# One PSUM pool of eight banks, half-size weight tiles and an earlier fourth weight sum in a transformer encoder block

## The chip, the cores and the metric

The kernel runs on one core of a Trainium2 chip. The metric is the device time of one execution in microseconds (us). Every number ahead of the prediction comes from the kernel before the change: from its three timed runs or from one execution taken by the hardware profiler. In the profile, PE is TensorE (matmuls), PEld its weight loads, DVE is VectorE, ACT is ScalarE, POOL is GpSimd and SP is the engine whose queue issues most DMAs. In the timeline each engine's instructions stand in the order of its program, so an instruction that waits holds up all that stand behind it on that engine.

## What is computed

One encoder block on 256 tokens of width 2048, in float32. What matters here is the tail of it and the matmul work:

```python
h = rms_norm(x, g_mix);  proj = h @ w_in            # q, k, v of three mixers, and three gates
...                                                 # three attentions; memory tokens: rms_norm(mem) @ w_mem_kv
merged = gates[0] * (oa @ w_br_a) + gates[1] * (ob @ w_br_b) + gates[2] * (oc @ w_br_c)
x = x + merged @ w_o
hf = rms_norm(x, g_ffn) @ w_ffn_in                  # 2048 x (2 * 5632)
x = x + (silu(hf[..., :D_FF]) * hf[..., D_FF:]) @ w_ffn_out
```

## The kernel before

Weights stream from HBM once, in tiles of up to 128 x 4 x 512 (`raw`, 1 MB, three slots). A float32 product is made from three matmuls on rounded halves: `split` lets ACT write the high part `whi` (line 86) and DVE the rest `wlo` (line 87) of a 128 x 2 x 512 half, and PE then adds high x high, high x low and low x high for each 128-row tile. `whi` and `wlo` have four slots each, so ACT runs at most four halves ahead of PE.

The stages follow each other on PE: two `w_mem` column blocks, eight `w_qkv` blocks with the attention heads worked in beside them (`tick` advances side jobs between matmuls), twelve pairs of gate and branch products with the merge, four `w_o` blocks, and the FFN. `product` (lines 161 to 188) makes one 512-wide column block into two PSUM banks, one per 128 tokens (`ps[0]`, `ps[1]`). `transposed` (lines 223 to 237) turns a finished block with eight PE transposes into two banks `tp` and splits the result for the next product.

The FFN's input product runs in eleven blocks through `in_seven` (lines 525 to 615). A block makes the two factors of 512 hidden columns for both token halves. For three pairs of k tiles (steps `s0` to `s2`) it uses seven products in place of eight, from sums of the weights (`t2`, `t3`, `t4`, made by DVE) and of the activations (`fh`, `fl`). The other five pairs (`d3` to `d7`) are done plainly. `ORDER` lists the steps of a block: `6`, `7` and `4` are the products with `t2`, `t3` and `t4`, over all three pairs at once. The partial sums are in banks X, Y, Z, W, V and Q. Y, V, Z and Q take the plain steps; X serves three sums one after the other, which ACT copies out. At a block's end DVE combines banks and copies into SA and SB (lines 609 to 614), ACT applies Silu (line 623), DVE multiplies (line 624), and `transposed` turns the product for `w_ffn_out`. A group of blocks (4, 4 and 3) is followed by four `w_ffn_out` products over that group, added to `x` (line 637).

PSUM has eight banks. Up to `w_o`, pool `mm` holds four (products) and pool `at` four (attention, transposes). For the FFN both are closed and opened anew as seven and one (lines 503 to 505).

The order of instructions on each engine is made by the framework's scheduler from program order and data dependencies. A tile gets one of its pool's slots as the scheduler places its first writer.

Of the kernel before, what the change touches and what calls it, by code (L numbers as in the profile page):

```python
# [11 lines left out]
F32 = mybir.dt.float32  # L12
# [15 lines left out]
PK, LOAD = 2, 4  # L28
# [24 lines left out]
ORDER = "s0 d3 s1 d4 s2 d5 6 d6 7 d7 4".split()  # L53
ORDER0 = "d3 d4 d5 s0 s1 d6 s2 6 d7 7 4".split()
# [3 lines left out]
def encoder_block(ctx: ExitStack, tc: tile.TileContext, a: dict, out: bass.AP):  # L58
# [7 lines left out]
    banks = ExitStack()  # L66
    pools = {"mm": banks.enter_context(tc.tile_pool(name="pmm", bufs=4, space=bass.MemoryType.PSUM)),
             "at": banks.enter_context(tc.tile_pool(name="pat", bufs=4, space=bass.MemoryType.PSUM))}
# [7 lines left out]
    def at_bank(name):  # L76
        return pools["at"].tile([P, NC], F32, name=name, tag="at")

    def mm_bank(name="mm"):
        return pools["mm"].tile([P, NC], F32, name=name, tag="mm")  # L80
# [69 lines left out]
    def load(src, k0, nk):  # L150

        raw = wp.tile([P, LOAD, NC], F32, name="raw")
        if nk % PK:
            c = k0 % PK * NC
            nc.sync.dma_start(out=raw[:, 0], in_=src[k0 // PK][:, c:c + NC])
        else:
            nc.sync.dma_start(out=raw[:, :nk].rearrange("p (u k) n -> p u (k n)", k=PK),
                              in_=src[k0 // PK:(k0 + nk) // PK].rearrange("u p n -> p u n"))
        return raw

    def product(src, lhs, nk, head=(), beside={}):


        ps = [mm_bank() for _ in range(T)]
        k0 = 0
        while k0 < nk:
            n = head[0] if head else min(LOAD, nk - k0)
# [5 lines left out]
            for b in range(0, n, PK):  # L173
                m = min(PK, n - b)
                hi = wp.tile([P, PK, NC], F32R, name="whi", bufs=4)
                lo = wp.tile([P, PK, NC], F32R, name="wlo", bufs=4)
                split(hi[:, :m], lo[:, :m], raw[:, b:b + m])
                for i in range(m):
                    k = k0 + b + i
                    xh, xl = lhs(k)  # L180
                    for t in range(T):
                        c = slice(t * P, (t + 1) * P)
                        nc.tensor.matmul(ps[t], lhsT=xh[:, c], rhs=hi[:, i], start=(k == 0), stop=False)  # L183
                        nc.tensor.matmul(ps[t], lhsT=xh[:, c], rhs=lo[:, i], start=False, stop=False)  # L184
                        nc.tensor.matmul(ps[t], lhsT=xl[:, c], rhs=hi[:, i], start=False, stop=(k == nk - 1))  # L185
                    tick()
            k0 += n
        return ps
# [34 lines left out]
    def transposed(src, dst, g=None):  # L223

        for h in range(2):
            tp = at_bank("tp")
# [40 lines left out]
    def biases():  # L267
# [7 lines left out]
        for g in range(3):  # L275
# [4 lines left out]
            ps = at_bank("bias_ps")  # L280
# [19 lines left out]
    def take_slots(ps, slots, r, name="x", eng=nc.gpsimd):  # L300
# [38 lines left out]
        if n:  # L339
# [14 lines left out]
            for j in range(n):  # L354
                tp = at_bank("hT")
# [10 lines left out]
    def attend(qs, ks, vs, bias, kt):  # L366
# [5 lines left out]
        for i in range(g):  # L372
            sc = at_bank("sc")
# [29 lines left out]
        def turn(i):  # L403
            tp = at_bank("pT")
# [9 lines left out]
        ops = at_bank("o")  # L414
# [27 lines left out]
    first = product(a["w_mem"][0], memT, KT, (1, 1) + (2,) * 7, {6: row_sums(a["mem"], r_m, 3, "mem")})  # L442
# [3 lines left out]
    start(take_slots(product(a["w_mem"][1], memT, KT, (2,) * 8), MEM_SLOTS[4:], r_m, "mem"))  # L446
# [78 lines left out]
    def in_seven(src, lhs, forms, order):  # L525
# [5 lines left out]
        dest = {"s": "XYZW", "6": "X", "7": "X", "4": "V"}  # L531
        left = {}
        for o in order:
            for b in ([dest["s"][0], "Y", "Z", "W"] if o[0] == "s" else ["Y", "V", "Z", "Q"] * 2 if o[0] == "d"
                      else [dest[o]] * SEVEN):
                left[b] = left.get(b, 0) + 1
# [4 lines left out]
        def mul(b, st, hi, lo):  # L541
            first = b not in ps
            if first:
                ps[b] = mm_bank("mm" + b)
# [7 lines left out]
        def halves():  # L552
            hi = wp.tile([P, PK, NC], F32R, name="whi", bufs=4)
            lo = wp.tile([P, PK, NC], F32R, name="wlo", bufs=4)
            return hi, lo
# [7 lines left out]
        t4 = s8([P, SEVEN, NC], "t4", F32)  # L563
        for o in order:
            if o[0] in "sd":
                u = int(o[1])
                raw = wp.tile([P, LOAD, NC], F32, name="raw")
                nc.sync.dma_start(out=raw.rearrange("p k n -> p (k n)"), in_=src[u])
            if o[0] == "d":
                for c in range(2):  # L570
                    hi, lo = halves()
                    split(hi, lo, raw[:, 2 * c:2 * c + 2])
# [4 lines left out]
            elif o[0] == "s":  # L577
                hi, lo = halves()
                split(hi, lo, raw[:, :2])
                mul("X", at(2 * u, 0), hi[:, 0], lo[:, 0])  # L580
                mul("Y", at(2 * u + 1, 0), hi[:, 1], lo[:, 1])
                hi, lo = halves()
                nc.vector.tensor_add(t3[:, u], raw[:, 2], raw[:, 3])
                nc.vector.tensor_add(raw[:, 2], raw[:, 2], raw[:, 0])
                split(hi, lo, raw[:, 2:])
                mul("W", forms(u, 0), hi[:, 0], lo[:, 0])
                mul("Z", forms(u, 2), hi[:, 1], lo[:, 1])
                nc.vector.tensor_add(t2[:, u], raw[:, 2], raw[:, 3])
                nc.vector.tensor_add(t4[:, u], t2[:, u], raw[:, 1])
                tick()  # L590
                if left["X"] == 2 * SEVEN:
                    nc.scalar.activation(SA[:, 0], ps["X"], AF.Copy)
                if left["W"] == 0:
                    nc.scalar.activation(SA[:, 1], ps["W"], AF.Copy)
            else:
                tt, f = {"6": (t2, 1), "7": (t3, 3), "4": (t4, None)}[o]
                for v in range(0, SEVEN, 2):
                    n = min(2, SEVEN - v)
                    hi, lo = halves()
                    split(hi[:, :n], lo[:, :n], tt[:, v:v + n])  # L600
                    for i in range(n):
                        u = v + i
                        mul(dest[o], at(2 * u + 1, 1) if f is None else forms(u, f), hi[:, i], lo[:, i])
                tick()
                if o == "6":
                    nc.scalar.activation(SB[:, 0], ps["X"], AF.Copy)
                elif o == "7":
                    nc.scalar.activation(SB[:, 1], ps["X"], AF.Copy)
        nc.vector.tensor_sub(SB[:, 0], SB[:, 0], SA[:, 1])
        nc.vector.tensor_sub(SA[:, 1], SA[:, 1], SB[:, 1])  # L610
        nc.vector.tensor_add(SA[:, 0], ps["Y"], SA[:, 0])
        nc.vector.tensor_add(SB[:, 1], ps["V"], SB[:, 1])
        nc.vector.tensor_sub(SB[:, 0], ps["Z"], SB[:, 0])
        nc.vector.tensor_add(SA[:, 1], ps["Q"], SA[:, 1])
        return (SA[:, 0], SB[:, 1]), (SB[:, 0], SA[:, 1])

    forms = stationary_forms()
    for c0, c1 in ((0, 4), (4, 8), (8, KF // 4)):
        hT = []
        for n in range(c0, c1):  # L620
            av, bv = in_seven(a["w_ffn"][n], x1l, forms, ORDER0 if n == 0 else ORDER)
            for t in range(T):
                nc.scalar.activation(av[t], av[t], AF.Silu, scale=r_f[:, 0, t:t + 1])
                nc.vector.scalar_tensor_tensor(av[t], bv[t], r_f[:, 0, t:t + 1], av[t],
                                               op0=ALU.mult, op1=ALU.mult)
            tl = s8([P, 2, 4, S], "hT", pool=tail)
            hT.append(tl)
            transposed(av, lambda k, m: (tl[:, 0, k:k + m], tl[:, 1, k:k + m]))
# [51 lines left out]

def _layout(i):
# [37 lines left out]
```

## Time and profile before

| | us |
|---|---|
| three timed runs, median (lowest to highest) | 1429.48 (1427.87 to 1429.51) |
| the profiled execution, its own time | 1432.02 |
| its span, first to last instruction | 1430.2 |
| PE busy in the span | 1400.4 |
| PE idle in the span | 29.8 |
| DVE, ACT busy | 963.3, 741.0 |

A group's row in the views gives the line, the engine, the operation, what is written from what, its shapes and its count; then busy time and mean duration in ns, and behind the bar the idle time of that engine just ahead of such instructions with what ended it. Matmuls overlap in the pipe: a 128x512 one is recorded with 389 ns while the next starts after some 228 ns, so spacing is read from starts. PEclk, or the granted clock, is the share of full speed that TensorE was given.

### The profile page before, as it was taken

What the parts mean: (1) busy time and instruction counts of PE and PEld (TensorE: products, weight loads), DVE (VectorE), ACT (ScalarE), POOL (GpSimd) and SP (SyncE); (2) the same over time, 40 slices, a digit from 0 to 9 for tenths busy, and PEclk for the clock granted to TensorE, in tenths of its full rate; (3) what the DMA queues carried; (4) which work ended last, traced back from release to release, by engine and by line L of the source; (5) the groups of instructions that cost most, each with busy time, mean ns of one, the idle gap of its engine ahead of it and who ended that gap; (6) DMA issues with size and microseconds to landing.
All of it is one profiled execution on the core that took longest, in us unless ns stands there. A gap on an engine that the chain in (4) does not pass through costs nothing.

```text
span 1430.2 us, 16503 instructions
## 1 busy us (share of the span) xinstructions
PE 1400.4 (98%) x6323; PEld 1151.6 (81%) x6323; DVE 963.3 (67%) x1191; ACT 741.0 (52%) x971; POOL 78.8 (6%) x146
## 2 busy tenths in 40 slices
PE   6999999999999999999899999999999999999998
PEld 4778788888888888888687788888888888888887
DVE  5666776754455555555688987557988855788763
ACT  5576556544444444444456555435655643456542
POOL 0012642200000000000000000000000000000000
PEclk8999999999999999999999999999999999999999
DMA  8876445456555555655455554555554555655562
GB/s 293 272 255 187 147 175 176 135 218 217 195 180 202 191 169 188 213 181 179 174 177 180 211 186 188 187 195 206 201 186 176 203 206 190 222 176 178 206 223 101
DMA packets 64510, 276.99 MB, mean 194 GB/s; under 512 B 5232, under 2 KB 7792, under 8 KB 52912
## 3 DMA queue, kind: packets, MB, share of 16 engines
q1 hardware_dynamic: 61984, 271.73, 54.8%
q10 hardware_dynamic: 2448, 4.22, 0.9%
q8 instruction: 49, 0.80, 0.2%
q14 instruction: 29, 0.24, 0.0%
HBM read 273.05 MB, written 2.88 MB: 193 GB/s over the span
## 4 chain that ended last, share of the span: by engine, by line
PE 89%; DMA 4%; POOL 2%; DVE 2%; ACT 2%; issue 1%; SPq 0%; ACTq 0%; DVEq 0%; POOLq 0%
PE mm L184 18%; PE mm L183 18%; PE mm L185 18%; PE mmY L549 2%; PE mmY L550 2%; PE mmY L548 2%; PE mmZ L549 2%; PE mmZ L550 2%; PE mmZ L548 2%; PE mmV L549 2%; PE mmV L550 2%; PE mmV L548 2%; PE mmQ L550 2%; PE mmQ L549 2%; PE mmQ L548 2%; PE mmX L549 1%
## 5 line engine op out<-in xcount | busy, mean ns | idle before, releaser
L87 DVE TENSOR_TENSOR wlo<-raw,whi 128x1024 fp32r<-128x1024 f32 (+1 forms) x497 | 612.6, 1238 | 393.4 <-ACT whi L86 392.1
L86 ACT ACTIVATE whi<-raw 128x1024 fp32r<-128x1024 f32 (+1 forms) x497 | 524.0, 1061 | 573.5 <-PE mm L185 367.1
L183 PE MATMUL mm<-whi,xT 128*128 128x512 f32 x640 | 250.6, 393 | 1.4 <-ACT whi L86 1.1
L184 PE MATMUL mm<-wlo,xT 128*128 128x512 f32 x640 | 250.2, 391 | 1.1 <-DVE wlo L87 1.1
L185 PE MATMUL mm<-whi,xT 128*128 128x512 f32 x640 | 249.5, 391 | 0.0
L183 PEld LDWEIGHTS mm<-whi,xT 128*128 128x128 f32 x640 | 120.1, 188 | 26.7 <-ACT whi L86 1.6
L184 PEld LDWEIGHTS mm<-wlo,xT 128*128 128x128 f32 x640 | 120.2, 188 | 26.3 <-DVE wlo L87 1.5
L185 PEld LDWEIGHTS mm<-whi,xT 128*128 128x128 f32 x640 | 120.2, 188 | 24.6
L184 PE MATMUL mm<-wlo,hT 128*128 128x512 f32 x352 | 138.0, 393 | 0.0
L185 PE MATMUL mm<-whi,hT 128*128 128x512 f32 x352 | 137.6, 393 | 0.0
L183 PE MATMUL mm<-whi,hT 128*128 128x512 f32 x352 | 134.9, 391 | 0.0
L184 PEld LDWEIGHTS mm<-wlo,hT 128*128 128x128 f32 x352 | 66.1, 188 | 14.8
L183 PEld LDWEIGHTS mm<-whi,hT 128*128 128x128 f32 x352 | 66.1, 188 | 14.6
L185 PEld LDWEIGHTS mm<-whi,hT 128*128 128x128 f32 x352 | 66.1, 188 | 13.6
L87 DVE TENSOR_TENSOR wlo<-t,whi 128x1024 fp32r<-128x1024 f32 x66 | 62.9, 955 | 6.3 <-ACT whi L86 3.6
L548 PE MATMUL mmY<-whi,x1T 128*128 128x512 f32 x143 | 57.7, 403 | 5.6 <-DVE rs_h L96 5.6
L86 ACT ACTIVATE whi<-t 128x1024 fp32r<-128x1024 f32 x66 | 55.6, 843 | 10.9 <-PE mmX L550 5.7
L549 PE MATMUL mmY<-wlo,x1T 128*128 128x512 f32 x143 | 56.7, 397 | 0.1
L550 PE MATMUL mmY<-whi,x1T 128*128 128x512 f32 x143 | 56.3, 393 | 0.0
L548 PE MATMUL mmV<-whi,x1T 128*128 128x512 f32 x143 | 56.2, 393 | 0.0
L549 PE MATMUL mmV<-wlo,x1T 128*128 128x512 f32 x143 | 55.9, 391 | 0.0
L550 PE MATMUL mmV<-whi,x1T 128*128 128x512 f32 x143 | 55.9, 391 | 0.0
(192 smaller groups left out, 2117.5 us busy)
## 6 DMA issues: line engine op xcount, KB each, us to landing
raw<-in_w_ffn SPq DMA_DIRECT2D x88, 1024.0 KB, 4.9
raw<-in_w_gate SPq DMA_DIRECT2D x48, 1024.0 KB, 5.0
raw<-in_w_ffn_out SPq DMA_DIRECT2D x44, 1024.0 KB, 5.0
raw<-in_w_qkv SPq DMA_DIRECT2D x32, 1024.0 KB, 5.0
raw<-in_w_o SPq DMA_DIRECT2D x16, 1024.0 KB, 4.9
raw<-in_w_br SPq DMA_DIRECT2D x8, 1024.0 KB, 5.0
raw<-in_w_mem SPq DMA_DIRECT2D x15, 512.0 KB, 4.7
raw<-in_w_br SPq DMA_DIRECT2D x8, 512.0 KB, 3.5
```

The costliest lines, as they stand in the source:

```text
L86: nc.scalar.activation(hi, src, AF.Copy)
L87: nc.vector.tensor_sub(lo, src, hi.bitcast(F32))
L183: nc.tensor.matmul(ps[t], lhsT=xh[:, c], rhs=hi[:, i], start=(k == 0), stop=False)
L184: nc.tensor.matmul(ps[t], lhsT=xh[:, c], rhs=lo[:, i], start=False, stop=False)
L185: nc.tensor.matmul(ps[t], lhsT=xl[:, c], rhs=hi[:, i], start=False, stop=(k == nk - 1))
L548: nc.tensor.matmul(ps[b], lhsT=st[0], rhs=hi, start=first, stop=False, skip_group_check=chain)
L549: nc.tensor.matmul(ps[b], lhsT=st[0], rhs=lo, start=False, stop=False, skip_group_check=chain)
L550: nc.tensor.matmul(ps[b], lhsT=st[1], rhs=hi, start=False, stop=stop, skip_group_check=chain)
```

## The change

* All stages draw from one PSUM pool of eight banks under one tag (`bank`). Closing and reopening pools ahead of the FFN goes.
* `raw` becomes a half tile (128 x 2 x 512, 0.5 MB) with six slots in place of three full ones; each load is a DMA of its own. The FFN weights are laid out so that both factors' halves alternate (`_pairs`).
* The product with the fourth weight sum (`t4` before, step `4` at a block's end) is made for each pair at once, in its `s` step, from a sum written over the raw weights. It goes into bank V. `t4` and step `4` go.
* W is copied to SB, the second X sum to SB, the third to SA; the six combinations change accordingly.
* The FFN's row scale `r_f` stays in Silu but leaves the product: `av * bv` is one 128 x 1024 multiplication over both token halves, and `r_f` is applied where the output products are added to `x`.

The core of the diff:

```diff
-ORDER = "s0 d3 s1 d4 s2 d5 6 d6 7 d7 4".split()
-ORDER0 = "d3 d4 d5 s0 s1 d6 s2 6 d7 7 4".split()
+ORDER = "s0 d3 s1 d4 s2 d5 6 d6 7 d7".split()
+ORDER0 = "d3 d4 d5 s0 s1 d6 s2 6 d7 7".split()
...
-    pools = {"mm": banks.enter_context(tc.tile_pool(name="pmm", bufs=4, space=bass.MemoryType.PSUM)),
-             "at": banks.enter_context(tc.tile_pool(name="pat", bufs=4, space=bass.MemoryType.PSUM))}
+    psum = ctx.enter_context(tc.tile_pool(name="psum", bufs=8, space=bass.MemoryType.PSUM))
...
+    def bank(name):
+        return psum.tile([P, NC], F32, name=name, tag="bank")
...
     def load(src, k0, nk):
-        raw = wp.tile([P, LOAD, NC], F32, name="raw")
...
+        raw = wp.tile([P, PK, NC], F32, name="raw", bufs=6)
+        c = k0 % PK * NC
+        nc.sync.dma_start(out=raw[:, :nk].rearrange("p k n -> p (k n)"), in_=src[k0 // PK][:, c:c + nk * NC])
...
-    banks.close()
-    pools["mm"] = ctx.enter_context(tc.tile_pool(name="pm2", bufs=7, space=bass.MemoryType.PSUM))
-    pools["at"] = ctx.enter_context(tc.tile_pool(name="pa2", bufs=1, space=bass.MemoryType.PSUM))
...
             elif o[0] == "s":
...
+                b1, b2 = raws
+                hi, lo = halves(b1)
                 mul("X", at(2 * u, 0), hi[:, 0], lo[:, 0])
                 mul("Y", at(2 * u + 1, 0), hi[:, 1], lo[:, 1])
...
-                nc.vector.tensor_add(t2[:, u], raw[:, 2], raw[:, 3])
-                nc.vector.tensor_add(t4[:, u], t2[:, u], raw[:, 1])
                 tick()
+                nc.vector.tensor_add(b1[:, 1], t2[:, u], b1[:, 1])
+                hi, lo = halves(b1[:, 1])
+                mul("V", at(2 * u + 1, 1), hi[:, 0], lo[:, 0])
...
         nc.vector.tensor_add(SA[:, 0], ps["Y"], SA[:, 0])
-        nc.vector.tensor_add(SB[:, 1], ps["V"], SB[:, 1])
+        nc.vector.tensor_sub(SB[:, 0], SB[:, 0], SB[:, 1])
         nc.vector.tensor_sub(SB[:, 0], ps["Z"], SB[:, 0])
-        nc.vector.tensor_add(SA[:, 1], ps["Q"], SA[:, 1])
-        return (SA[:, 0], SB[:, 1]), (SB[:, 0], SA[:, 1])
+        nc.vector.tensor_sub(SB[:, 1], SB[:, 1], SA[:, 1])
+        nc.vector.tensor_add(SB[:, 1], ps["Q"], SB[:, 1])
+        nc.vector.tensor_add(SA[:, 1], ps["V"], SA[:, 1])
+        return SA, SB
...
             for t in range(T):
-                nc.scalar.activation(av[t], av[t], AF.Silu, scale=r_f[:, 0, t:t + 1])
-                nc.vector.scalar_tensor_tensor(av[t], bv[t], r_f[:, 0, t:t + 1], av[t],
-                                               op0=ALU.mult, op1=ALU.mult)
+                nc.scalar.activation(av[:, t], av[:, t], AF.Silu, scale=r_f[:, 0, t:t + 1])
+            nc.vector.tensor_mul(av, av, bv)
...
-                    nc.vector.tensor_add(x[t][:, o], op[t][:, h * w:(h + 1) * w], x[t][:, o])
+                    nc.vector.scalar_tensor_tensor(x[t][:, o], op[t][:, h * w:(h + 1) * w], r_f[:, 0, t:t + 1],
+                                                   x[t][:, o], op0=ALU.mult, op1=ALU.add)
```

The scheduler moves more than the diff shows. On PE, at the end of the second FFN block, before the change (mmX to mmQ are the banks, `tp` the transposes of the finished block, `fh` the summed activations; the first row is the last one of step `4`):

```order
L550 MATMUL mmV<-whi,x1T 128x512
L548 MATMUL mmX<-whi,x1T 128x512
L548 MATMUL mmY<-whi,x1T 128x512
L549 MATMUL mmX<-wlo,x1T 128x512
L550 MATMUL mmX<-whi,x1T 128x512
L549 MATMUL mmY<-wlo,x1T 128x512
L550 MATMUL mmY<-whi,x1T 128x512
L548 MATMUL mmW<-whi,fh 128x512
L548 MATMUL mmZ<-whi,fh 128x512
L548 MATMUL mmY<-whi,x1T 128x512
L548 MATMUL mmV<-whi,x1T 128x512
L229 MATMUL tp<-ident,SA 128x128
```

The same place on PE in the changed program:

```order
L532 MATMUL mmQ<-whi,x1T 128x512
L533 MATMUL mmQ<-wlo,x1T 128x512
L534 MATMUL mmQ<-whi,x1T 128x512
L218 MATMUL tp<-ident,SA 128x128 x8
L532 MATMUL mmX<-whi,x1T 128x512
L533 MATMUL mmX<-wlo,x1T 128x512
L534 MATMUL mmX<-whi,x1T 128x512
```

All eight transposes stand right behind the block's last matmul, and the next block's first matmul stands behind them. Before, ten matmuls of the next block stood ahead of the first transpose, and the other seven came 35 to 77 rows after it. The other ten blocks show the same, and so do the ends of the merge and `w_o` products, where two transposes now stand right behind the last matmul.

On DVE, the rows of the changed program that lead to the multiplication of that block (`SA<-SA,SB`, which the transposes read; `t_6698` and `t_6699` are sums of the next block, and the rows on `raw` prepare the next block too):

```order
L592 TENSOR_TENSOR SB<-SB,SA 128x512
L573 TENSOR_TENSOR raw<-t_6698,raw 128x512
L82 TENSOR_TENSOR wlo<-raw,whi 128x1024
L589 TENSOR_TENSOR SA<-mmY,SA 128x512
L594 TENSOR_TENSOR SA<-mmV,SA 128x512
L599 TENSOR_TENSOR t_6699<-raw 128x512
L82 TENSOR_TENSOR wlo<-raw,whi 128x512
L591 TENSOR_TENSOR SB<-mmZ,SB 128x512
L593 TENSOR_TENSOR SB<-mmQ,SB 128x512
L600 TENSOR_TENSOR raw<-raw 128x512
L82 TENSOR_TENSOR wlo<-raw,whi 128x1024
L610 TENSOR_TENSOR SA<-SA,SB 128x1024
```

Six of the twelve are work for the next block; three of those are splits of its weights. Before, the two multiplications of a block stood apart, each behind its own half.

At the entry to the FFN, PE before had the whole last transposition of `w_o` and then the first FFN matmul:

```order
L185 MATMUL mm<-whi,mT 128x512
L229 MATMUL tp<-ident,x_5087 128x128 x2
L229 MATMUL tp<-ident,x_5088 128x128
L229 MATMUL tp<-ident,x_5087 128x128
L229 MATMUL tp<-ident,x_5088 128x128 x2
L229 MATMUL tp<-ident,x_5087 128x128
L229 MATMUL tp<-ident,x_5088 128x128
L548 MATMUL mmY<-whi,x1T 128x512
```

and in the changed program:

```order
L174 MATMUL mm<-whi,mT 128x512
L218 MATMUL tp<-ident,x_5260 128x128 x2
L532 MATMUL mmY<-whi,x1T 128x512
L533 MATMUL mmY<-wlo,x1T 128x512
L534 MATMUL mmY<-whi,x1T 128x512
```

Twenty FFN matmuls now stand between the second transpose and the other six.

More of the change, by code (lines that the diff above doesn't have):

```diff
@@ L172, in product @@
             raw = load(src, k0, n)
[L173 to L186, printed above, removed]
+            hi = wp.tile([P, PK, NC], F32R, name="whi", bufs=4)
+            lo = wp.tile([P, PK, NC], F32R, name="wlo", bufs=4)
+            split(hi[:, :n], lo[:, :n], raw[:, :n])
+            for i in range(n):
+                k = k0 + i
+                xh, xl = lhs(k)
+                for t in range(T):
+                    c = slice(t * P, (t + 1) * P)
+                    nc.tensor.matmul(ps[t], lhsT=xh[:, c], rhs=hi[:, i], start=(k == 0), stop=False)
+                    nc.tensor.matmul(ps[t], lhsT=xh[:, c], rhs=lo[:, i], start=False, stop=False)
+                    nc.tensor.matmul(ps[t], lhsT=xl[:, c], rhs=hi[:, i], start=False, stop=(k == nk - 1))
+                tick()
             k0 += n
@@ L413, in attend @@
         turn(0)
-        ops = at_bank("o")
+        ops = bank("o")
         for i in range(g):
@@ L441, in encoder_block @@
     memT(0)
-    first = product(a["w_mem"][0], memT, KT, (1, 1) + (2,) * 7, {6: row_sums(a["mem"], r_m, 3, "mem")})
+    first = product(a["w_mem"][0], memT, KT, (1, 1), {6: row_sums(a["mem"], r_m, 3, "mem")})
     start(constants())
```

88 lines of the change are left out of this document (36 added, 52 removed).

## The prediction

> **What bounds the kernel now.** I read the page's first part, then its chain of work that ended last.
>
> ```profile
> PE 1400.4 (98%) x6323; PEld 1151.6 (81%) x6323; DVE 963.3 (67%) x1191; ACT 741.0 (52%) x971; POOL 78.8 (6%) x146
> ...
> PE 89%; DMA 4%; POOL 2%; DVE 2%; ACT 2%; issue 1%; SPq 0%; ACTq 0%; DVEq 0%; POOLq 0%
> ```
>
> PE is busy for 1400.4 of 1430.2 us and carries 89% of the chain. The change keeps the number of matmuls and transposes, so what it can move is PE's stalls: 29.8 us now, and whatever it adds. The timeline of PE around the end of `w_o` gives the spacing and the largest stall that the change touches (start, duration, and in brackets the idle time before).
>
> ```profile
> 700.01 0.39 PE L185 MATMUL mm<-whi,mT 128*128 128x512 f32 x1
> ...
> 702.98 0.39 PE L183 MATMUL mm<-whi,mT 128*128 128x512 f32 x1
> ...
> 703.44 0.39 PE L185 MATMUL mm<-whi,mT 128*128 128x512 f32 x1
> 704.10 0.44 PE L229 MATMUL tp<-ident,x 128*128 128x128 f32 x2 [0.27 <-DVE x L492]
> 704.69 0.87 PE L229 MATMUL tp<-ident,x 128*128 128x128 f32 x6 [0.16 <-DVE x L492]
> 711.18 0.77 PE L548 MATMUL mmY<-whi,x1T 128*128 128x512 f32 x1 [5.61 <-DVE rs_h L96]
> ```
>
> From 700.01 to 702.98 there are 13 steps: 0.228 us from one matmul to the next, though one lasts 0.39. The stall ahead of the FFN is 5.61 us. Next the stretches view (busy PE, PEld, DVE, ACT, POOL; then granted clock, DMA share, GB/s), for an FFN block, that stall, what follows it, and the program's start.
>
> ```profile
> 757.00:799.50 42.50, 41.59 (x187) 34.02 (x186) 36.06 (x43) 25.20 (x30) 0.00 (x0) 1.00 0.56 198
> 705.50:711.20 5.70, 0.09 (x2) 0.05 (x1) 5.70 (x14) 2.23 (x7) 0.00 (x0) 0.77 0.56 184
> 711.20:715.40 4.20, 4.20 (x10) 3.37 (x11) 3.86 (x12) 1.48 (x1) 0.00 (x0) 0.50 0.00 0
> 0.00:18.00 18.00, 7.12 (x24) 5.36 (x24) 4.44 (x11) 10.01 (x18) 0.70 (x6) 0.94 0.89 333
> 20.00:26.00 6.00, 5.64 (x13) 4.03 (x14) 4.87 (x17) 3.15 (x6) 0.00 (x0) 0.51 0.65 208
> ```
>
> Inside a block PE hardly stalls, and DVE (36.06 of 42.5) and ACT are within it. After the stall PE had half its clock for 4.2 us: 10 matmuls where 0.228 each would be 2.3, so 1.9 us more were lost.
>
> **The change, term by term.** The order on each engine decides, and it moves against PE.
>
> *1. Block ends of the FFN, eleven times.* All eight transposes now stand between a block's last matmul and the next block's first one. They read `SA`, which DVE multiplies only after bank Q, finished by that last matmul, was added. I take this to come from the one pool: `tp` precedes the next block's banks in the program. Whatever the reason, PE has nothing to do until that multiplication is done. DVE's prices:
>
> ```profile
> 798.51 0.68 DVE L613 TENSOR_TENSOR SB<-mmZ,SB 128x512 f32<-128x512 f32 x1
> 799.11 0.68 DVE L614 TENSOR_TENSOR SA<-mmQ,SA 128x512 f32<-128x512 f32 x1
> 799.71 0.68 DVE L584 TENSOR_TENSOR raw<-raw 128x512 f32<-128x512 f32 x1
> ...
> 804.43 2.36 DVE L87 TENSOR_TENSOR wlo<-raw,whi 128x1024 fp32r<-128x1024 f32 x2
> ```
>
> and, by line and form, a 1024-wide DVE step on plain float32 (the longer of line 516's two) and ACT's steps (min, median and max in ns, or busy us and mean):
>
> ```profile
> L516 DVE TENSOR_TENSOR ffull<-x1T x2: 684/952/1219, 706.1 to 707.2; 128x1024 f32<-128x1024 f32 x1, 128x512 f32<-128x512 f32 x1
> ```
>
> ```profile
> L592 ACT ACTIVATE SA<-mmX x11: 577/578/598, 742.0 to 1335.1; 128x512 f32<-128x512 f32 x11
> ...
> L623 ACT ACTIVATE SA<-SA,scales x11: 707/707/724, 751.0 to 1355.4; 128x512 f32<-128x512 f32 x11
> ```
>
> ```profile
> L86 ACT ACTIVATE whi<-raw 128x1024 fp32r<-128x1024 f32 x495 | 522.8, 1062 | 571.9 <-PE mm L185 367.1 <-PE mmQ L550 81.8 <-PE mmV L550 60.0
> ```
>
> Queued behind one another, a 512-wide step takes 0.60 us (798.51, 799.11, 799.71), a 1024-wide split 1.18 and the last 1024-wide multiplication 1.22. Call the start of the last matmul 0. DVE cannot run ahead freely: the split just before the twelve rows shown in the change (the next block's first half) needs the `whi` slot of the product with `t3`, whose last matmul stands 27 steps back, starts at -6.2 and ends at -5.8; ACT needs 1.06, DVE 1.24, so DVE enters the twelve rows at -3.5. They are nine of 0.60, two of 1.18 and the multiplication: 9.0 us. The first transpose can start at 5.5 in place of 0.23: a stall of **5.3 us**. Nothing covers it, since PE takes its queue in order. From below, with DVE waiting for Q: 0.39 for the matmul, then the last four rows, 0.60 + 0.60 + 1.18 + 1.22, less 0.23, is 3.8. From above, a late slot could add the 1.0 that ACT takes for one more half: 6.3. I take 5.3, since every wait in it is read from a row; seven blocks are of this kind.
>
> The last block of each group (three) has four rows less for the next block in that list and two splits more: by the same counting DVE enters at -3.4 and has six steps of 0.60, two splits behind ACT's Silus and the multiplication; transposes at about 4.4, stall 4.1. The first block ends with bank X: ACT copies it (0.58), DVE subtracts, splits twice (0.60, 1.18), adds Q and V, ACT applies Silu (0.71), DVE multiplies: 0.39 + 0.58 + 0.60 + 0.60 + 1.18 + 1.20 + 0.71 + 1.22 = 6.5, and some 0.7 for ACT's own splits between, less 0.23: 7.0. Sum: 7 x 5.3 + 3 x 4.1 + 7.0 = **+56.4** (11 x 3.8 = 42 to 11 x 6.3 = 69).
>
> *2. The clock after these stalls.* In the stretches above, the 5.6 us stall cost 1.9 us more. I charge 1.9 for the eight of 5.3 and over, and half for the three of 4.1, which no row shows: 15.2 + 2.9 = **+18** (0 to 11 x 3.0 = 33; 3.0 from 20 to 26 us, where 13 matmuls took 6.0 us). The Trainium skill, "TensorE: Matmul & The Clock Gate", section "Why this matters for your kernels", says that gaps over about 3 us bring the clock back to half. The trace agrees for the 5.61 us gap, and by that rule alone all eleven would be charged: 21 in place of 18.
>
> *3. Entry to the FFN.* No pool is closed, and twenty matmuls on earlier k tiles stand behind two transposes. The 5.61 goes and the 1.9 with it: **-7.5**. Next late are the last x1T splits and `fh`, needed only some 70 matmuls (16 us) on. From the other side, -5.6.
>
> *4. Ends of the merge and `w_o` products.* The transposes move up in the same way.
>
> ```profile
> L475 DVE TENSOR_TENSOR sg<-mm,sg x16: 679/683/684, 407.8 to 612.5; 128x512 f32<-128x512 f32 x16
> L476 DVE TENSOR_TENSOR mg<-mg,sg x16: 680/684/689, 409.0 to 613.7; 128x512 f32<-128x512 f32 x16
> ```
>
> ```profile
> L624 DVE SCALAR_TENSOR_TENSOR SB<-SA,scales,SB 128x512 f32<-128x512 f32 x11 | 8.2, 750 | 0.0
> ...
> L229 PE MATMUL tp<-ident,mg 128*128 128x128 f32 x32 | 4.8, 272 | 0.0
> ```
>
> Merge transposes waited 0.0 with 27 matmuls ahead. Now they wait for both multiplications and an addition: 0.39 + 0.60 + 0.68 - 0.23 = 1.4, four times. At `w_o` the stall is the 0.27 and 0.16 seen at 704, for three blocks more: 1.3. **+6.9** (3 to 10).
>
> *5. The first heads, at 62 us.* Their eight transposes moved ahead of the first `w_qkv` product; before, sixteen matmuls stood there.
>
> ```profile
> 62.62 0.50 PE L183 MATMUL mm<-whi,xT 128*128 128x512 f32 x1 [0.22 <-ACT y L324]
> ...
> 63.68 2.41 POOL L331 TENSOR_TENSOR y<-y,gh 128x1024 f32<-128x1024 f32 x1 [62.37 <-ACT y L324]
> ```
>
> If POOL is as late, PE waits from 62.4 to 66.1, 3.7 us; if ACT reaches it earlier, for its splits of `w_qkv` now stand behind, nothing. I take the middle: **+2** (0 to 3.7).
>
> *6. Edits at nothing.* The start: PE's 13.4 us there end on ACT.
>
> ```profile
> L183 PE MATMUL mm<-whi,memT 128*128 128x512 f32 x64 | 26.1, 420 | 13.4 <-ACT memT L89 13.4
> ```
>
> ACT still stands in row order behind the squares of `mem`, whose DMAs now share the queue with deeper weight loads, so I take 0 (-7 if the stall at 13 to 20 us goes, +3). Attention's moved rows: 0 (-2 to +3). `r_f` on the output sum and the wider multiplication: DVE's, within the 6 us per block that it has free while PE works; without that cover the 24 output sums would add 24 x 0.066 = 1.6 (750 ns for the form with a scale, line 624 above, against 684). Smaller halves of the fourth sum: DVE and ACT take a few overheads more, in the same cover.
>
> *Sum.* 56.4 + 18 - 7.5 + 6.9 + 2 = +75.8. The profiled execution's own time, 1432.0, becomes 1507.8; it lies 2.5 above the median of the three runs, 1429.5, so I forecast **1505**.
>
> **Rivals.**
>
> *Stalls of the bare chain, clock unharmed.* DVE waits for Q with nothing queued, and the phase of the clock's control spares most stalls: 42 + 0 - 5.6 + 3 = +39: 1469. For it: DVE has 6 us free in 42.5. Against: the slots of `whi` hold DVE's entry at -3.5.
>
> *Block ends cost nothing: no slower.* Were the multiplication done by the time of the last matmul, terms 1 and 2 would vanish and +1.4 be left: 1431; with the start's 7 us gone, 1424. It decides at a stall of 0.6 us per block (6.9 over eleven). The idle 0.0 of the merge's transposes speaks for it, but there other matmuls stood ahead; Q's addition and the multiplication alone are 0.39 + 0.60 + 1.22 - 0.23 = 2.0 us behind the last matmul.
>
> *Half-size loads starve PE.* Rows of DMA issues (KB each, us to landing):
>
> ```profile
> raw<-in_w_ffn SPq DMA_DIRECT2D x88, 1024.0 KB, 4.9
> raw<-in_w_gate SPq DMA_DIRECT2D x48, 1024.0 KB, 5.0
> ...
> raw<-in_w_mem SPq DMA_DIRECT2D x15, 512.0 KB, 4.7
> raw<-in_w_br SPq DMA_DIRECT2D x8, 512.0 KB, 3.5
> ```
>
> One at a time, two halves take 7.0 where the 24 matmuls on them take 5.5: 1.5 us late for each full tile, 204 us over the 88 + 48 of the FFN's input and the gates alone, near 1634. It decides at fewer than 1.3 loads in flight; six slots are there, and the first 18 us, with `w_mem` in loads of 512 KB, moved 333 GB/s against 198 in a block. The Trainium skill, "DMA: Bandwidth & Descriptors", section "Bandwidth", advises 1 MiB and more per DMA; by that rule the halves lose rate, and these rows say that enough is left.
>
> *The change doesn't do what it says.* The stall at the FFN's entry stays because x1T is late: the forecast plus 7.5, 1513, within the range.
>
> **How the numbers follow.** Forecast with its bounds 0.73, bare chain 0.17, late entry 0.04; no cost at block ends 0.05, starved 0.01. The low end is the bare chain less 3 for attention and start: 1466. The high end is 69 + 33 - 5.6 + 10 + 3.7 = +110, which gives 1540; I take 1535, since these extremes hardly meet. Faster by over 0.2% (the least that a measurement of this kernel tells from no change, 2.9 us): 0.03, from the start gaining with free block ends; within: 0.02; slower: 0.95.
>
> **What would show it.** Right: idle of 4 to 7 us ahead of `tp<-SA`, released by DVE's multiplication, eleven times; clock dips in the FFN; no stall at its entry; `tp<-mg` idle of some 6 us. Wrong: `tp<-SA` idle under 2 us a block; granted clock staying 1.0; PE waiting for `raw` DMAs.

## The result, and the profile after

The changed kernel takes **1534.6 us** (median of four runs, 1534.19 to 1535.03) beside 1429.33 before (now four runs): a ratio of 1.0739, 95% interval 1.072 to 1.0758. That is 105.3 us more, where the forecast was 75.5 more (1505). The stated range, 1466 to 1535, holds it by 0.4 us.

The page of the changed kernel, PE's busy time and the chain that ended last:

```profile
PE 1429.8 (93%) x6323; PEld 1169.9 (76%) x6323; DVE 968.2 (63%) x1191; ACT 743.3 (49%) x982; POOL 78.7 (5%) x146
...
PE 78%; DVE 9%; DMA 5%; issue 3%; ACT 3%; POOL 1%; SPq 0%; DVEq 0%; ACTq 0%; POOLq 0%
```

PE has the same 6323 instructions, but is "busy" 29.4 us longer, mostly because a matmul on a slower clock is recorded as longer work (0.63 us in place of 0.39 in the rows below). Its share of the chain falls from 89% to 78%, and DVE's rises from 2% to 9%. Who keeps PE waiting stands in its waits (total us, times, longest):

```profile
PE tp L218 <- DVE SA L610: 56.4, 11, 8.4
PE mm L172 <- ACT memT L84: 18.7, 4, 9.6
PE hT L346 <- POOL y L320: 6.0, 1, 6.0
PE tp L218 <- DVE mg L465: 6.0, 4, 1.5
```

The first row is the step the forecast rested on: eleven stalls ahead of `tp<-SA`, 56.4 us in all. Before, these transposes waited once:

```profile
PE tp L229 <- DVE SA L624: 0.2, 1, 0.2
```

Here is one of the eleven, at the end of the second FFN block, on PE (start, duration, in brackets the idle time before):

```profile
831.02 0.39 PE L534 MATMUL mmQ<-whi,x1T 128*128 128x512 f32 x1
836.69 1.94 PE L218 MATMUL tp<-ident,SA 128*128 128x128 f32 x8 [5.28 <-DVE SA L610]
838.28 0.78 PE L532 MATMUL mmX<-whi,x1T 128*128 128x512 f32 x1
838.86 0.63 PE L533 MATMUL mmX<-wlo,x1T 128*128 128x512 f32 x1
...
841.85 0.46 PE L534 MATMUL mmW<-whi,fl 128*128 128x512 f32 x1
842.14 0.40 PE L532 MATMUL mmZ<-whi,fh 128*128 128x512 f32 x1
```

and what DVE did meanwhile:

```profile
827.56 0.68 DVE L592 TENSOR_TENSOR SB<-SB,SA 128x512 f32<-128x512 f32 x1
...
833.00 0.68 DVE L593 TENSOR_TENSOR SB<-mmQ,SB 128x512 f32<-128x512 f32 x1
833.60 0.68 DVE L600 TENSOR_TENSOR raw<-raw 128x512 f32<-128x512 f32 x1
834.19 1.22 DVE L82 TENSOR_TENSOR wlo<-raw,whi 128x1024 fp32r<-128x1024 f32 x1
835.33 1.22 DVE L610 TENSOR_TENSOR SA<-SA,SB 128x1024 f32<-128x1024 f32 x1
```

DVE enters the twelve rows 3.46 us ahead of PE's last matmul, never waits, and ends the multiplication 5.53 behind it. After the stall the matmuls start 0.43 us apart instead of 0.228, until about 842. The stretch behind it, with the granted clock third from the end:

```profile
836.70:842.00 5.30, 5.30 (x17) 4.53 (x18) 1.83 (x3) 1.92 (x3) 0.00 (x0) 0.50 0.22 87
```

To compare kernels stage by stage I add up PE's lost time from its timeline: the spacing of starts beyond 0.2275 us for a 512-wide matmul, 0.117 for a 256-wide one and 0.11 for a transpose. It counts idle time and slow clock alike. "First heads" are the 12 us behind the last matmul on `memT`; the FFN's entry ends 12 us ahead of its first transpose.

| lost us | before | after | difference | forecast |
|---|---|---|---|---|
| start (`w_mem`) | 12.6 | 21.6 | +9.0 | 0 |
| first heads | 1.9 | 7.5 | +5.6 | +2 |
| attention | 6.7 | 7.2 | +0.5 | 0 |
| merge and `w_o` | -0.3 | 8.0 | +8.3 | +6.9 |
| FFN entry | 8.3 | 7.9 | -0.4 | -7.5 |
| rest of FFN | 4.6 | 82.7 | +78.1 | +56.4 + 18 |
| sum | 33.7 | 134.9 | +101.2 | +75.8 |

The spans differ by 1532.1 - 1430.2 = 101.9, so the table misses almost nothing. The medians differ by 105.3, since the profiled execution before lay 2.7 us above its median and the one after 0.4 below.

### The profile page after: what moved, and what is told of

It is laid out like the page before. It is cut to its first block, busy times and chain, and to the rows that moved or that the text cites. A ratio compares the mean times of both kernels' runs of the same rounds, so it can differ in the third digit from the quotient of the medians.

```text
span 1532.1 us, 17228 instructions
## 1 busy us (share of the span) xinstructions
PE 1429.8 (93%) x6323; PEld 1169.9 (76%) x6323; DVE 968.2 (63%) x1191; ACT 743.3 (49%) x982; POOL 78.7 (5%) x146
## 4 chain that ended last, share of the span: by engine, by line
PE 78%; DVE 9%; DMA 5%; issue 3%; ACT 3%; POOL 1%; SPq 0%; DVEq 0%; ACTq 0%; POOLq 0%
PE mm L172 17%; PE mm L174 17%; PE mm L173 17%; DVE wlo L82 4%; ACT whi L81 2%; PE tp L218 2%; PE mmY L533 2%; PE mmY L534 2%; PE mmY L532 2%; DMA raw<-in_w_ffn 2%; PE mmZ L532 2%; PE mmV L534 2%; PE mmZ L533 2%; PE mmV L533 2%; PE mmZ L534 2%
## 5 line engine op out<-in xcount | busy, mean ns | idle before, releaser
L82 DVE TENSOR_TENSOR wlo<-raw,whi 128x1024 fp32r<-128x1024 f32 (+1 forms) x530 | 634.0, 1204 | 450.4 <-ACT whi L81 446.9
L81 ACT ACTIVATE whi<-raw 128x1024 fp32r<-128x1024 f32 (+1 forms) x530 | 542.8, 1032 | 615.1 <-PE mm L174 389.7
L174 PE MATMUL mm<-whi,hT 128*128 128x512 f32 x352 | 140.0, 398 | 0.0
L172 PE MATMUL mm<-whi,hT 128*128 128x512 f32 x352 | 139.6, 397 | 0.0
L218 PE MATMUL tp<-ident,SA 128*128 128x128 f32 x88 | 19.1, 390 | 56.4 <-DVE SA L610 56.4
L218 PEld LDWEIGHTS tp<-ident,SA 128*128 128x128 f32 x88 | 15.3, 203 | 60.8 <-issue 49.8
```

Of the source, the lines that this page charges most:

```text
L81: nc.scalar.activation(hi, src, AF.Copy)
L82: nc.vector.tensor_sub(lo, src, hi.bitcast(F32))
L218: nc.tensor.transpose(tp[:, k * S + t * P:k * S + (t + 1) * P], src[t][:, (2 * h + k) * P:(2 * h + k + 1) * P], ident)
```

## The experiments

All times are medians; "before" was timed beside each set (1429.14, 1429.91 and 1429.23 us). Theory A: the single tag makes the transposes stand at block ends, DVE's queue sets how long PE waits there, and the clock falls behind each wait. The rivals blame the new arithmetic, or the half tiles.

**1. The changed kernel, transposes in a bank of their own.**

```diff
-psum = tile_pool(name="psum", bufs=8, ...)
+psum = tile_pool(name="psum", bufs=7, ...)
-            tp = bank("tp")
+            tp = psum.tile([P, NC], F32, name="tp", tag="tp", bufs=1)
```

> The changed kernel with one edit: seven banks under the tag bank, and one bank under a tag of its own for the transposes of finished blocks (merge, w_o and FFN). All of the arithmetic and the half tiles stay. Theory A (the one tag puts the transposes ahead of the next block's matmuls): in the new order some 50 matmuls of the next block stand ahead of the first transpose, so the idle ahead of them (56.4 us in the changed kernel's profile), the 22.7 us lost in the 8 us behind these stalls and the 6.0 us ahead of the merge's transposes go: 1534.6 - 85 = 1450 us, between 1445 and 1465. Rival B (the wide multiplication and the new order of the sums stall PE in any pool, since Q is added last in both): still 1520 to 1535 us, with idle on some other instruction at block ends.

1452.3 us (ratio 1.0164, 1.0147 to 1.0181). No wait on `tp` is left; the rest of the FFN loses 5.0 us, merge and `w_o` -0.4. One tag was worth 82 us. Of the 23 that remain, the profiled execution (19.5 in its span) has 18.4 at the start (19.5 us lost, before 12.6), the first heads (8.5, before 1.9) and attention (11.6, before 6.7).

**2. The kernel before with one pool alone.**

```diff
-pools = {"mm": ... bufs=4 ..., "at": ... bufs=4 ...}
+psum = tile_pool(name="psum", bufs=8, ...)     # all banks: tag="bank"
-banks.close(); pools["mm"] = ... bufs=7; pools["at"] = ... bufs=1
```

> The kernel before with one edit: one pool of eight banks under one tag for all stages; full tiles, fourth sum at the block's end and two multiplications per block stay. In its order two transposes (of the half that does not need bank V) stand right behind the block's last matmul and six stand some 45 rows later. Theory A1 (the pool decides where the transposes stand, but how long they wait is set by the DVE queue ahead of the multiplication): Q is done 9 matmuls before the block's end and one 512-wide multiplication is enough for the two, so a wait of 0 to 3 us per block, about 2: +25 for eleven blocks with little loss of clock, +7 for the merge, -7.5 for the entry to the FFN, +4 for the first heads: 1440 to 1465 us, about 1458. Rival A2 (the pool alone makes the whole loss): 1505 to 1535. Rival C (the pool alone costs nothing, the loss needs the new arithmetic): 1420 to 1431.

1442.97 us (1.0099, 1.0083 to 1.0114): A1, at its low end. The waits of `tp`:

```profile
PE tp L227 <- DVE SA L619: 7.4, 7, 1.5
PE tp L227 <- DVE mg L474: 6.0, 4, 1.5
```

Seven stalls of about 1 us with no clock lost behind them. (Theory A1 gave the block ends 25 us of this; 7.4 came.) So the pool is needed for the loss, but does not make it alone: 13.8 us against 82.

**3. The changed kernel, stalls filled with matmuls** that serve nothing (nothing reads what they write; the code in short, with `v` for bank V).

```diff
+            seed = flx[:, 15]
+            nc.scalar.activation(seed, v[:, :P], AF.Copy)       # v: bank V
...
             tp = bank("tp")
+            for _ in range(24 if n == 0 else 16):               # first half only
+                nc.tensor.matmul(tp, lhsT=seed, rhs=x1T[0][:, 0, 0:2], start=True, stop=True)
```

> The changed kernel with work added: 24 (first block) and 16 (ten others) extra matmuls 128x512, 184 in all, on no data that is used, into the bank of the transposes, right ahead of the transposes at a block's end; they wait for a small ACT copy of bank V (128x128), so that they stand in the stall. The output stays the reference's. Clock theory (what is lost behind each stall is half clock, granted down because PE stood still): with PE idle for at most some 2 us in a piece, the granted clock stays 1.0 behind the stalls and most of the 22.7 us come back although 184 matmuls (42 us of PE) were added: 1512 to 1524 us. Rival (the loss behind the stalls is restart latency, or the stalls are set by PE's own work): the added matmuls lengthen the program or leave it the same: 1534 us or more.

1515.82 us (1.0604, 1.0589 to 1.062): 184 matmuls more, 18.8 us less. PE's timeline at the same block end:

```profile
833.92 0.39 PE L537 MATMUL mmQ<-whi,x1T 128*128 128x512 f32 x1
835.67 3.92 PE L217 MATMUL tp<-x1T,fl 128*128 128x512 f32 x16 [1.36 <-ACT fl L612]
839.43 1.08 PE L220 MATMUL tp<-ident,SA 128*128 128x128 f32 x8
840.26 0.47 PE L535 MATMUL mmX<-whi,x1T 128*128 128x512 f32 x1
840.57 0.39 PE L536 MATMUL mmX<-wlo,x1T 128*128 128x512 f32 x1
840.80 0.39 PE L537 MATMUL mmX<-whi,x1T 128*128 128x512 f32 x1
```

and the stretch behind the stall:

```profile
839.40:844.00 4.60, 4.60 (x25) 3.94 (x25) 2.77 (x4) 2.80 (x4) 0.00 (x0) 1.00 0.28 109
```

The transposes still go 5.5 us behind the last matmul, as DVE dictates, but the clock stays 1.00 and the next matmuls are 0.23 apart. In the 8 us behind each of the eleven stalls the changed kernel lost 22.7 us in all; here it loses about half a microsecond. (In the first block 6.41 us still pass before the added matmuls, and it is they that run on the lower clock.) The loss behind a stall is the clock, and idle PE is what brings it down.

**4. The kernel before with half tiles, six slots.**

```diff
-raw = wp.tile([P, LOAD, NC], F32, name="raw")                 # three slots of 1 MB
+raw = wp.tile([P, PK, NC], F32, name="raw", bufs=6)           # six of 0.5 MB, a DMA each
```

> The kernel before with one edit: weights in half tiles with six slots, each load a DMA of its own of 512 KB; pools and arithmetic stay. Theory (the six slots let more weight loads stand in the queue ahead of the rows of mem, memT and xT, so these land later and PE waits more at the start): the changed kernel lost about 8.6 us more up to 60 us than the kernel before, and I expect that loss here, and nothing in the FFN: 1429.4 + 6 to 10 = 1436 to 1440 us. Rival (the later start in the changed kernel comes from ACT's order under the one pool, not from the loads): 1428 to 1431. Rival (512 KB loads are too slow for PE): above 1450, with PE waiting for raw DMAs in the FFN.

1453.18 us (1.0169, 1.0154 to 1.0184). That misses the 1436 to 1440 expected. The start loses 22.5 us, as expected; the expectation of nothing in the FFN was wrong: its rest loses 16.0 instead of 4.6. The time lies where the second rival put it, above 1450. PE itself waits for no `raw` DMA there, but a weight sum of DVE's does (before, then this run):

```profile
DVE t L583 <- DMA raw<-in_w_ffn: 6.0, 12, 1.8
DVE t L582 <- DMA raw<-in_w_ffn: 51.5, 28, 4.7
```

Whether these waits cost PE the 11 us is not shown: in run 1, with the new arithmetic, DVE waits 27.9 us in the same way and the rest of the FFN loses 5.0. The cause of this part stays open.

**5, 6, 7. The changed kernel's arithmetic, undone one at a time and together** (one pool and half tiles stay).

```diff
-            nc.vector.tensor_mul(av, av, bv)                     # run 5 and 7
+            for t in range(T):
+                nc.vector.tensor_mul(av[:, t], av[:, t], bv[:, t])
```

```diff
-ORDER = "s0 d3 s1 d4 s2 d5 6 d6 7 d7".split()                   # run 6 and 7
+ORDER = "s0 d3 s1 d4 s2 d5 6 d6 7 d7 4".split()                 # ORDER0 too
-                nc.vector.tensor_add(b1[:, 1], t2[:, u], b1[:, 1])
-                hi, lo = halves(b1[:, 1])
-                mul("V", at(2 * u + 1, 1), hi[:, 0], lo[:, 0])
+                nc.vector.tensor_add(t4[:, u], t2[:, u], b1[:, 1])   # multiplied in step "4"
```

> The changed kernel with one edit: two multiplications 128x512, one per token half, in place of the one of 128x1024 (one pool and the fourth sum used at once stay). In its order two transposes stand ahead of the next block's first matmul instead of eight; on DVE both multiplications still stand behind the addition of Q, a sum and a split for the next block. Theory Q (the queue on DVE sets the stall; the width adds only its own second half): the first transposes can go 0.6 us earlier, 11 x 0.6 = 7 us, and up to 5 more from shorter stalls with less loss of clock: 1522 to 1529 us. Rival W (the wide multiplication is what ties all eight transposes to the block's last bank, and with halves most of the stall goes): 1455 to 1475.

> The changed kernel with one edit: the fourth weight sum is kept and multiplied at the block's end, into bank V, as in the kernel before (one pool, half tiles and the wide multiplication stay). Nine matmuls (2.05 us) then stand behind bank Q, but the wide multiplication needs V as well. Theory Q (whatever the last bank, the wide multiplication waits for it and for the rows ahead of it on DVE; eight transposes stand at the block's end): stalls of 5 to 7 us again, 1530 to 1555 us. Rival F (using the fourth sum at once is what uncovered the block's end): the nine matmuls hide some 2 us per block, with less loss of clock: 1490 to 1515.

> The changed kernel with both edits: the fourth weight sum at the block's end and two multiplications of 128x512 (one pool, half tiles and the row scale on the output sum stay). The two transposes at a block's end then need only the half without bank V, and nine matmuls cover the addition of Q and that multiplication. Theory Q with both parts needed: stalls of about 1 us per block as in the kernel before with one pool (7.4 us of idle in all), so that kernel's 1443 us and the 23 us that half tiles cost in the kernel before: 1460 to 1470. Rival (the stall is the one pool's whatever the arithmetic does with half tiles): above 1500.

1513.31 us (1.0586, 1.0568 to 1.0605), 1543.25 (1.0786, 1.077 to 1.0802) and 1456.91 (1.0188, 1.0173 to 1.0203, some 3 us under the range expected). The waits of `tp` in the three, in this order:

```profile
PE tp L218 <- DVE SA L611: 42.0, 11, 4.7
```

```profile
PE tp L218 <- DVE SA L610: 70.0, 11, 9.5
```

```profile
PE tp L218 <- DVE SA L611: 6.0, 7, 0.9
```

Run 5 gained 21 us where theory Q said 6 to 13. Its ordinary blocks behave as Q says (4.66 us in place of 5.19, since the first half's multiplication ends 0.6 earlier); the last block of a group fell further, from 3.92 to 2.25, and the first from 8.44 to 2.86, more than Q gives: there the halves did part of what rival W says. Run 6 is slower than the changed kernel: the nine matmuls of step `4` cover nothing, because the wide multiplication waits for V, which they finish. Together the two edits take 78 us off, singly they give -21 and +9. With one tag the block's end is safe only if a multiplication can finish early: halves alone leave the last banks, Z and Q, at the very end, and the late fourth sum alone leaves the wide multiplication waiting for V. So the loss needs the one tag (run 1) and a chain at the block's end that nothing covers (run 7), and the forecast, which read the chain rightly, gave only the pool as the reason for the order.

**8. Half tiles with three slots instead of six** (kernel before).

```diff
-raw = wp.tile([P, PK, NC], F32, name="raw", bufs=6)
+raw = wp.tile([P, PK, NC], F32, name="raw", bufs=3)
```

> The kernel before with half tiles, as in the run on half tiles with six slots, but three slots of 512 KB: at the start, where the kernel before also had loads of 512 KB, there are three in flight as before. Theory (the depth of six slots delays memT and rows at the start): the stall at 13 us returns from 9.0 to about 7 us and the excess up to 62 us from 22.5 to about 13; behind the start PE may wait for raw DMAs, since one load takes 3.6 us to land and three of them feed a half every 2.73 us only if a slot is held under 8.2 us: 1445 to 1500 us. Rival (the size of the tiles or the order, not the depth, makes the late start): the start stays at 9 us and some 22 us of excess.

1511.35 us (1.0572, 1.0543 to 1.0601), above the 1445 to 1500 expected. The start is back: 12.0 us lost. The loads of `w_mem` have 512 KB in all these kernels; their median time to landing is 4.7 before, and in the changed kernel (its other ACT load beside it)

```profile
raw<-in_w_mem SPq DMA_DIRECT2D x15, 512.0 KB, 7.1
rawT<-in_memT ACTq DMA_DIRECT2D x8, 256.0 KB, 4.9
```

and with three half slots

```profile
raw<-in_w_mem SPq DMA_DIRECT2D x15, 512.0 KB, 4.8
```

So it is the depth: six loads under way instead of three take longer each, and ACT stands longer in `rows` and `memT`. Behind the start, three half slots starve PE through ACT (ACT's own waits):

```profile
ACT whi L86 <- DMA raw<-in_w_ffn: 110.5, 59, 4.1
```

and the rest of the FFN loses 79.7 us. Three half slots are too few there, and six too many at the start.

**9. Run 1 with full tiles and three slots again.**

```diff
+        raw = wp.tile([P, 2 * PK, NC], F32, name="raw", bufs=3)      # loads and product as before
...
-                raws = [load(src, 2 * (2 * u + c), PK) for c in range(2)]
+                raw = load(src, 4 * u, 2 * PK)
+                raws = [raw[:, :PK], raw[:, PK:]]
```

> The changed kernel with the transposes in a bank of their own (as in the first run: seven banks and one) and with weights in full tiles of 1 MB with three slots again; the fourth sum used at once, the wide multiplication and the row scale on the output sum stay. Theory (the 23 us by which the run with an own bank stays behind the kernel before are the half tiles', and the new arithmetic is worth nothing to PE, which waited for none of it): 1452 less 9 us at the start and 4 to 6 at the first heads: 1433 to 1440 us, not below the kernel before. Rival (the new arithmetic frees DVE and gains once the banks and tiles are right): below 1425. Rival (half tiles were not what cost): 1448 to 1455.

1444.48 us (1.0102, 1.0089 to 1.0116): 7.8 us less than run 1 and 15 more than before, above the 1433 to 1440 expected and below the rival that cleared the half tiles. Start (12.5) and first heads (2.7) are back, as expected; attention now loses 15.6 instead of 6.7, which I had not expected. Run 1 has it too (11.6), the kernels with eight banks under the tag do not (7.2 to 7.5): the heads draw from seven banks here, and I take that for the cause, though no run varies it alone. The new arithmetic gains nothing (rest of the FFN 8.6, before 4.6).

**10. The kernel before, both pools kept open for the FFN.**

```diff
-    banks = ExitStack()
+    banks = ctx
-    banks.close()
-    pools["mm"] = ...; pools["at"] = ...
-                ps[b] = mm_bank("mm" + b)
+                ps[b] = (at_bank if b in "VQ" else mm_bank)("mm" + b)
```

> The kernel before with one edit: its two pools of four banks are kept open for the FFN; X, Y, Z and W take banks of the first, V, Q and the transposes banks of the second. In its order two transposes stand four matmuls into the next block, so nine matmuls of the fourth sum and these four cover the chain from Q. Theory (the wait at the entry to the FFN, 5.6 us plus 1.9 of clock, was the closing of the pools; in the one-pool version of the kernel before, about 4 of these 7.5 us were saved): 1422 to 1427 us. Rival (the second pool's ring ties the transposes to bank V and gives the gain back at eleven block ends): 1428 to 1440.

**1423.37 us** (0.996, 0.9947 to 0.9972): the one version that beats both kernels, 5.9 us under the one before. The FFN's entry loses 3.3 instead of 8.3; PE's longest waits are

```profile
PE mm L183 <- ACT memT L89: 12.2, 3, 5.9
PE hT L357 <- POOL rot L351: 1.8, 2, 1.4
PE mmW L545 <- ACT whi L86: 1.5, 1, 1.5
```

The 5.6 us of the entry are gone from the list, and `tp` is not in its upper rows.

**11. Run 10 with later row sums of `mem`.**

```diff
-    first = product(..., {6: row_sums(a["mem"], r_m, 3, "mem")})
+    first = product(..., {14: row_sums(a["mem"], r_m, 3, "mem")})
```

> As the run with both pools kept, and the row sums of mem started behind the 14th k tile of the first product in place of the 6th, so that three of the four squares and their loads stand behind the last memT tiles on ACT and on the queue. Theory (PE's 7.0 us stall at 13 us is ACT standing in the squares while their rows land): the stall falls to under 2 us and the run is 4 to 8 us faster than the one with pools kept: 1415 to 1421. Rival (the loads of 512 KB themselves are late there, or the row scale now arrives late for the first heads): no faster, 1422 to 1430.

1428.6 us (0.9996, 0.9987 to 1.0005): 5 us slower than run 10.

```profile
PE mm L183 <- ACT memT L89: 8.1, 2, 5.9
PE mm L183 <- DVE V L90: 6.7, 1, 6.7
```

This is the rival's case. The stall at 13 us, 5.88 in run 10, fell to 2.27 (the other wait in the first row is PE's very first, 5.85), but the row scale is late now: at 59 us PE waits 6.7 us for DVE's scaling of `V`, which needs that scale and holds the banks that PE is to write next. The stall was moved and grew.

## Why the prediction was right, and where it was not

**Block ends (+56.4 forecast): right.** 56.4 us of idle in eleven stalls. The single sizes: 5.10 to 5.28 where 5.3 was worked out, 3.92 for 4.1, and 8.44 for 7.0 in the first block. The two sums agree to the digit partly because these errors cancel. The cause was stated as taken, not known ("I take this to come from the one pool"): run 1 shows it, and runs 2 and 5 to 7 that the pool needs the arithmetic as well, which the prediction left open.

**Clock (+18): right, somewhat low.** 22.7 us behind the eleven stalls: 1.4 to 2.8 each where 1.9 was charged, and 1.65 behind those of 3.92, where I had charged half of 1.9 (the last section says why they spread). The rule of the Trainium skill ("TensorE: Matmul & The Clock Gate", section "Why this matters for your kernels": gaps over about 3 us bring half clock) would have charged all eleven, 21, and was the nearer one. Run 3 shows that the clock is the whole of it.

**FFN entry (-7.5): the step that failed most**, -0.4. The stall went, as the step said. Wrong was to charge nothing for what comes next: "next late are the last x1T splits and `fh`, needed only some 70 matmuls (16 us) on". These were ready in time, but DVE, busy with them, came late to the first weight sums, and PE waited for those some 20 us on (the first FFN matmul starts at 728.7). PE of the changed kernel there:

```profile
746.97 0.39 PE L534 MATMUL mmY<-whi,x1T 128*128 128x512 f32 x1
748.33 0.50 PE L532 MATMUL mmW<-whi,fh 128*128 128x512 f32 x1 [0.97 <-ACT whi L81]
748.67 0.40 PE L532 MATMUL mmZ<-whi,fh 128*128 128x512 f32 x1
750.04 0.80 PE L533 MATMUL mmW<-wlo,fh 128*128 128x512 f32 x1 [0.98 <-DVE wlo L82]
750.64 0.63 PE L534 MATMUL mmW<-whi,fl 128*128 128x512 f32 x1
```

and two of DVE's rows:

```profile
743.49 1.76 DVE L82 TENSOR_TENSOR fl<-fraw,fh 128x1536 fp32r<-128x1536 f32 x1 [1.55 <-ACT fh L81]
...
746.36 1.29 DVE L600 TENSOR_TENSOR raw<-raw 128x512 f32<-128x512 f32 x2
```

Sums of the activations that DVE had made in the stall now stand in front of the first weight sums. The runs split it: with the pools unclosed and the fourth sum at the end the entry loses 3.3 to 4.1 (runs 2, 6, 7, 10, 11), with the fourth sum at once 7.1 to 8.4 (the changed kernel, runs 1, 5 and 9). Not closing the pools gave some 4 to 5 us, and using the fourth sum at once took some 4 back.

**Start (0): mis-sized**, +9.0. The reason was named ("whose DMAs now share the queue with deeper weight loads") but valued at nothing, with +3 as its bound. Runs 4 and 8 show it: 22.5 us lost with six slots, 12.0 with three.

**First heads (+2): mis-sized**, +5.6, above the bound of 3.7, which took POOL to be as late as before. It was later: ACT, behind `xT` tiles whose loads landed late, scaled `y` 1.7 us behind the last matmul on `memT`; before it did so 0.6 us ahead of it. One pool with full tiles loses 2.3 there (run 2), half tiles with two pools 3.1 (run 4), both together 7.5 to 8.7: the two edits meet in one place, and I had priced them apart.

**Merge and `w_o` (+6.9): right**, +8.3, of it 6.0 ahead of `tp<-mg`: four stalls of 1.49 where 1.4 was worked out.

**Rivals.** Bare chain (1469) fell: DVE never waits in the twelve rows. Free block ends fell. Half-size loads that starve PE: not with six slots in the changed kernel, whose upper waits name no `raw` DMA; run 8 shows the starving with three, and run 4 leaves 11 us open. The range held the time, but only through its upper bounds for other terms than the ones that moved: the sum was 25 us short, of which entry, start and first heads are 7.1 + 9.0 + 3.6 and the clock 4. That the time still fell inside, by 0.4 us, is in good part luck.

## What to carry to other kernels

When buffers of several kinds share one ring, the order in which they are asked for can become the order on the engine that writes them, as it did on PE in runs 1 and 2: before merging pools, look at what will stand behind the slowest of them, and give short-lived tiles that wait for another engine a ring of their own. A stall of 5 us on TensorE cost 5 here and then 1.4 to 2.8 more in clock; count both. And a stall that is removed is worth only what the next late thing leaves of it: the one at the FFN's entry came back in part 20 us on in the changed kernel, the one at 13 us came back at 59 us in run 11.

## What the runs showed of the hardware

When does a gap on TensorE cost clock? In run 5 nothing was lost behind gaps of 2.25 us, at the ends of the groups,

```profile
926.43 0.41 PE L218 MATMUL tp<-ident,SA 128*128 128x128 f32 x2 [2.25 <-DVE SA L611]
926.59 0.48 PE L172 MATMUL mm<-whi,hT 128*128 128x512 f32 x1
926.91 0.40 PE L173 MATMUL mm<-wlo,hT 128*128 128x512 f32 x1
```

but 1.7 us behind the one of 2.86 us at the end of the first block, with 0.43 between starts behind it:

```profile
781.01 0.41 PE L218 MATMUL tp<-ident,SA 128*128 128x128 f32 x2 [2.86 <-DVE SA L611]
781.18 0.48 PE L532 MATMUL mmX<-whi,x1T 128*128 128x512 f32 x1
...
782.27 0.63 PE L532 MATMUL mmY<-whi,x1T 128*128 128x512 f32 x1
```

The length of the gap is not the rule. In each of the thirteen profiles the granted clock changes only on a grid of 3.41 us, and it stays at 0.50 for one to three steps of it. Here is run 5 cut along its grid, two steps at the first block's end and two at the group's (busy PE, PEld, DVE, ACT, POOL; then granted clock, DMA share, GB/s):

```profile
778.17:781.58 3.41, 0.57 (x4) 0.55 (x5) 3.41 (x6) 2.06 (x3) 0.00 (x0) 1.00 0.14 10
781.58:784.99 3.41, 3.41 (x10) 2.67 (x9) 3.41 (x6) 1.06 (x1) 0.00 (x0) 0.50 0.73 223
...
921.52:924.93 3.41, 2.65 (x12) 1.88 (x10) 3.41 (x5) 3.04 (x4) 0.00 (x0) 1.00 0.86 287
924.94:928.35 3.41, 1.92 (x10) 1.65 (x11) 3.08 (x5) 0.38 (x1) 0.00 (x0) 1.00 0.64 223
```

The gap of 2.86 us lies within one step, and the next step has half the clock. The gap of 2.25 us is spread over two, and the clock stays. Counted by the spacing of starts over all thirteen profiles, each fall of the clock followed a step of which PE left at least 1.9 us unfilled, and after each step at full clock with more than 2.2 us unfilled it fell. Two gaps can add up: at the FFN's entry of the changed kernel (rows at 748 above) 0.97 us and most of 0.98 us lie in one step, and the 0.63 rows follow. It also says why gaps of 3.92 to 9.52 us (the changed kernel and run 6) were followed by losses of 1.4 to 2.9 us in no order of their length: what is lost is half of the slow time that lies behind the gap, and the grid decides how much that is. Behind the stall that ends at 836.69 the clock was slow until 841.95, 5.26 us, and 2.6 us were lost.
